# Two query tiles exchanged, the output projection's first part paced ahead of the attention, samples prepared beside the last head with their outputs outside the page pool

## The chip, the cores and the metric

The kernel runs as one program on 1 core of a Trainium2 chip. The metric is the device time of one execution in microseconds (us). TensorE (PE, with its weight loads PEld), VectorE (DVE), ScalarE (ACT), GpSimd (POOL) and SyncE (SP) each work through their own list of instructions in the order in which the program was written, and wait on semaphores for one another. SP issues most of the DMA transfers, ACT and POOL issue a few.

## The reference

One inference step of a two-layer hybrid encoder. Each layer projects its input, runs three mixers side by side (multi-head latent attention, an mLSTM and a gated delta net), gates their outputs, and projects the concatenation back:

```
proj = rms_norm(x, norm_w) @ w_in
q = (rms_norm(c_q, q_norm) @ w_uq).reshape(B, L, MLA_HEADS, MLA_NOPE + MLA_ROPE)
q_nope, q_rope = q[..., :MLA_NOPE], apply_rope(q[..., MLA_NOPE:], pos)
c_new = rms_norm(c_kv, kv_norm); kr_new = apply_rope(k_r, pos)
...
if absorbed:  q_lat = einsum('blhd,rhd->blhr', q_nope, w_uk)          # samples
else:         k_nope = einsum('bkr,rhd->bkhd', c_kv, w_uk); v = einsum('bkr,rhd->bkhd', c_kv, w_uv)   # prompt
p = softmax(where(mask, (q_rope·k_rope + q·k) * scale, -inf)) ; o = p · v   (samples: p · c_kv, then w_uv)
...
mixed = concatenate([o_a * silu(z_a), o_m * silu(z_m), o_g * silu(z_g)], axis=-1)
return x + mixed @ w_out, ...
```

There is one prompt of 16 + 1024 frames and there are 8 sample streams of 16 new frames, each with a cache of 1040 latent rows of 256 numbers and 1040 rope keys of 32. The 8 heads have 64 plain ("nope") and 32 rotated ("rope") query dimensions. Arithmetic is float32; products are made from a high and a low part of each operand, three matmuls for one.

## The kernel before, in words

All activations stand transposed, 1168 columns (1040 of the prompt, 128 of the samples) in three slices. SBUF is mostly a pool of 28 numbered "pages" (tiles named `pg`, 128 x 1168 float32 or thereabouts); smaller tiles (`wk`, `sm`) have pools of their own. PSUM has two pools, `pa` of 3 and `pb` of 5 buffers. `room(n)` asks whether n pages are free.

The order of all instructions is made when the program is built, by a planner (class `Weave`). A main thread writes the projections, then `qkv`, then `out_first` and `out_proj`; side threads (`prep`, `gload`, `att_m`, `att`, `samp_*`) yield either a time in planner microseconds after which they are resumed, or the name of an event that they wait for. When no side thread is due, the main thread writes its next piece, so its matmuls fill the places between the side threads' steps. A changed pause, page count or event therefore moves instructions on all engines.

Per layer, in the places that the change touches:

- `qkv`: `qtile(j)` makes the query tiles. Tiles 0 and 3 hold rope dimensions of four heads each: DVE multiplies the PSUM result with the two halves of a rotation table `tabq` (L1420, L1423), POOL adds them (L1425), SP writes 8 pieces to the scratch tensor `qS` in DRAM (L1435). Tiles 1, 2, 4 and 5 hold nope dimensions: ACT scales them out of PSUM (L1427), SP writes two pieces (L1438). Tile 0 comes first, then tile 1, then the four key tiles, written to `kS` by slices (L1458, L1459), then the values. `load` (L453) fetches the next weights `wuv` or `wuq`, which ACT and then DVE or POOL split (L437, L441). The event `("qt", g)` lets the side thread `gload` fetch a head's queries and keys from `qS` and `kS` (L383, tiles `pg`) and ACT and POOL or DVE split them (L1529, L1530).
- `att` goes over 8 heads, 3 query slices and up to 9 key blocks. A step is three score matmuls, an exponential on ACT (L1589) and, three steps later, the product with the values (PV) into a `pa` buffer. At the end of a slice DVE forms the reciprocal of the denominator (L1612) and multiplies by the gate (L1613), POOL multiplies the two (L1614), and ACT issues the store of the 64 x 320 or 64 x 384 result to the scratch tensor `mix` (L1616). Each step yields `YX` = 0.35.
- `out_first` is the output projection's part for four of the twelve tiles of `mix`: 8 blocks of rows by 3 slices, 12 matmuls each. It is the main thread's work while the attention runs.
- `samp_prep` waits for the eighth head's queries and keys (event `("grp", 7)`) and 9 free pages, turns the samples' queries into the latent space (16 matmuls and 16 splits with DVE subtractions L441, after the rope part L1645 and L1646), and takes two pages `OL` for the samples' outputs.
- For each of 8 samples b: `samp_load` fetches the transposed latent (2 pages `latT`, 520 KB each) and the rope keys `krT`, three copies in 96 rows (390 KB); `samp_split` splits them (ACT L1697, L1700; DVE and POOL L1698, DVE L1701); `samp_ln` fetches the latent once more, rows first (`latN`, two pages of 512 KB, after the small `latE` and `tok` pieces, L383); `samp_s` makes scores (21 matmuls of 352 columns), their extremes (DVE L1744) and exponentials (ACT L1752); `samp_t` transposes these (9 transposes at L372, copied out at L1776 and L1783) and multiplies by `latN` (36 matmuls, "PV of a sample"). The result is copied to `OL` at L1795.
- `samp_out` turns `OL` into the samples' attention output, and `out_proj` does the remaining eight tiles of the output projection.

A DMA instruction waits, beside its data, for the transfer that used its semaphore slot before it: hardware-queue transfers go through eight slots (`DMAHW0` to `DMAHW7`) in turn. A transfer whose slot is still taken holds SP, and all that SP has to issue after it.

Of the kernel before, what the change touches and what calls it, by code (L numbers as in the profile page):

```python
# [42 lines left out]
YM_, YX, YR, YD = 0.5, 0.35, 2.4, 2.6  # L43
# [111 lines left out]
def pack(i):  # L155
# [52 lines left out]
    a["krT"] = f(np.concatenate([kr.transpose(0, 1, 3, 2)] * 3, 2))  # L208
# [99 lines left out]
def _build(nc, tc, ctx, I, O, layers):  # L308
# [278 lines left out]
    def layer(l, XH, XLp, XL, xres, xw, R):  # L587
# [797 lines left out]
        def qkv():  # L1385
# [19 lines left out]
            def qtile(j, wh, wl):  # L1405
# [25 lines left out]
                if j in (0, 3):  # L1431
                    for h in range(4):
                        for x_ in range(2):
                            o = 64 * x_ + 16 * h
                            QE.dma_start(qS[4 * (j // 3) + h, 64 + 16 * x_:80 + 16 * x_], sg[o:o + 16, :T])  # L1435
                else:
                    for h in range(2):
                        QE.dma_start(qS[2 * gr + h, 0:64], sg[64 * h:64 * h + 64, :T])  # L1438
                    D1["qt", gr] = 1
                free(sg)  # L1440

            (wh, wl), nxt = nxt, load("k")
            yield from qtile(0, wh, wl)
            yield from qtile(1, wh, wl)
# [122 lines left out]
        def att():  # L1567
            steps = [(h, s_, j) for h in range(8) for s_ in range(3) for j in range(9) if QB[j] < QS_[s_][1]]
            fly, po, zt = [], None, {}
            for i_ in range(len(steps) + LA):  # L1570
# [46 lines left out]
                yield YX  # L1617
# [8 lines left out]
        def samp_prep():  # L1626
            yield "qs"
            yield ("grp", 7)
            while not room(9):
                yield 7.08  # L1630
# [10 lines left out]
            for a in range(2):  # L1641
# [4 lines left out]
                V.tensor_sub(dst[64:96], src[64:96], dst[64:96].bitcast(F32))  # L1646
# [14 lines left out]
            A["OL"] = [pg() for _ in range(2)]  # L1661
# [4 lines left out]
        def samp_load():  # L1666
            yield "sprep"
            fly = A["fly"] = []
            for b in range(8):
                for k in range(3):  # L1670
# [4 lines left out]
                    p_, src = (slice(0, 128), I["latT"][l, b, :, k]) if k < 2 else (slice(0, 96), I["krT"][l, b])  # L1675
# [5 lines left out]
        def samp_split():  # L1681
            for b in range(8):
                out = []
                for k in range(3):
# [9 lines left out]
                    for s0 in (0, 528):  # L1694
# [4 lines left out]
                        else:  # L1699
                            gate(S.copy(hi[0:96, sl], raw[0:96, sl]))  # L1700
                            V.tensor_sub(hi[32:64, sl], raw[32:64, sl], hi[32:64, sl].bitcast(F32))  # L1701
# [59 lines left out]
        def samp_t():  # L1761
            for b in range(8):
# [31 lines left out]
                for r in range(2):  # L1794
                    (S.copy if r else V.tensor_copy)(  # L1795
                        A["OL"][r][:, :1024].rearrange("p (h b l) -> p h b l", h=8, b=8)[:, :, b, :],
                        po[:, 128 * r:128 * r + 128].rearrange("p (h l) -> p h l", l=16))
# [3 lines left out]
        def samp_out():  # L1801
# [21 lines left out]
            for pr in range(4):  # L1823
                ps = pb()
                for j in range(2):
                    h = 2 * pr + j
                    for r in range(2):
                        mm(ps[64 * j:64 * j + 64, 0:128], wuv[:, 512 * r + 64 * h:512 * r + 64 * h + 64],
                           OL[r][:, 128 * h:128 * h + 128], r == 0, r == 1)
# [3 lines left out]
            free(wuv, zs, *OL)  # L1833
# [35 lines left out]
        def out_first():  # L1869
# [22 lines left out]
            for a, b_ in mx:  # L1892
                free(a, b_)

# [96 lines left out]
```

## Time and profile before

| | |
|---|---|
| median of 3 runs | 2653.65 us (2650.51 to 2656.03) |
| profiled execution, its own time | 2655.11 us |
| its span in the profile | 2653.3 us |
| TensorE's mean granted clock | 0.976 of 2.4 GHz |
| PE busy | 2494.3 us, 94% |
| PEld, DVE, ACT, POOL busy | 81%, 58%, 42%, 29% |
| moved by DMA | 258.67 MB, mean 97 GB/s |

The profiled execution is 1.46 us longer than the median, and 1.8 us of its time lie outside the span. PE is busy nearly throughout, so what another engine costs shows as a gap in PE's row; each gap carries the instruction that ended it. Layer 0's attention ends at about 1137 us of the span, layer 1's at about 2440 us. PE's busy time also grows when its clock is granted at the lower of its two levels, 1.2 instead of 2.4 GHz; the windows show this as a mean clock under 1.00, where a window of 20 us at clock c holds (1 - c) x 20 us of lost time.

### The profile page before, as it was taken

What the parts mean: (1) busy time and instruction counts of PE and PEld (TensorE: products, weight loads), DVE (VectorE), ACT (ScalarE), POOL (GpSimd) and SP (SyncE); (2) the same over time, 40 slices, a digit from 0 to 9 for tenths busy, and PEclk for the clock granted to TensorE, in tenths of its full rate; (3) what the DMA queues carried; (4) which work ended last, traced back from release to release, by engine and by line L of the source; (5) the groups of instructions that cost most, each with busy time, mean ns of one, the idle gap of its engine ahead of it and who ended that gap; (6) DMA issues with size and microseconds to landing.
All of it is one profiled execution on the core that took longest, in us unless ns stands there. A gap on an engine that the chain in (4) does not pass through costs nothing. (4 is left out here: it accounts for less than half of the span.)

```text
span 2653.3 us, 45522 instructions
## 1 busy us (share of the span) xinstructions
PE 2494.3 (94%) x17310; PEld 2154.2 (81%) x17310; DVE 1529.8 (58%) x3716; ACT 1115.5 (42%) x2635; POOL 763.2 (29%) x865
## 2 busy tenths in 40 slices
PE   6999999999999999979998999999999999999997
PEld 4887888878878888779977888788788788887896
DVE  6667465465453476655565784755743526665636
ACT  5363444444442433443343544444444434334612
POOL 3112222122123542232341222221221245322414
PEclk9999999999999999989999999999999999998998
DMA  3212112121113734464422121221211255444832
GB/s 130 67 40 76 51 52 83 51 69 49 60 59 113 201 105 122 124 215 160 153 79 57 43 74 52 61 73 51 69 52 57 84 148 162 116 115 149 281 117 80
DMA packets 158411, 258.67 MB, mean 97 GB/s; under 512 B 48704, under 2 KB 110768, under 8 KB 158192
## 3 DMA queue, kind: packets, MB, share of 16 engines
q1 hardware_dynamic: 152224, 247.59, 30.2%
q0 software_dynamic: 1856, 3.86, 0.7%
q10 hardware_dynamic: 4112, 4.30, 0.7%
q8 instruction: 137, 2.24, 0.4%
q14 instruction: 82, 0.67, 0.1%
HBM read 190.77 MB, written 64.92 MB: 96 GB/s over the span
## 5 line engine op out<-in xcount | busy, mean ns | idle before, releaser
L361 PE MATMUL pa<-pg,wh 128*128 128x384 f32 (+3 forms) x6324 | 1320.5, 352 | 25.5 <-DVE wk L1423 8.8
L361 PEld LDWEIGHTS pa<-pg,wh 128*128 128x128 f32 x6324 | 1108.2, 190 | 69.4 <-DVE wk L1423 9.4
L361 PE MATMUL pb<-pg,pg 128*128 128x352 f32 (+26 forms) x1908 | 427.4, 339 | 17.7 <-DVE sm L1552 4.4
L361 PE MATMUL pa<-pg,wb 128*128 128x384 bf16 (+1 forms) x2208 | 422.1, 331 | 6.2 <-POOL pg L544 4.2
L361 PEld LDWEIGHTS pb<-pg,pg 128*128 128x128 f32 (+7 forms) x1908 | 302.5, 189 | 71.1 <-issue 14.9
L361 PEld LDWEIGHTS <-wb 128*128 128x128 bf16 x2208 | 202.0, 98 | 142.4 <-issue 30.4
L361 PE MATMUL pb<-wk,pg 128*128 128x128 f32 (+4 forms) x2168 | 224.2, 250 | 21.2 <-ACT wk L983 5.5
L441 POOL TENSOR_TENSOR wh<-wf,wh 128x1024 fp32r<-128x1024 f32 (+1 forms) x61 | 144.1, 2363 | 325.1 <-ACT wh L437 318.7
L361 PEld LDWEIGHTS pb<-wk,pg 128*128 128x128 f32 (+3 forms) x2168 | 195.2, 162 | 43.0 <-issue 16.8
L1589 ACT ACTIVATE wk<-pb 128x320 f32<-128x320 f32 (+8 forms) x288 | 113.9, 406 | 244.9 <-PE pb L361 221.4
L361 PE MATMUL pa<-wk,pg 128*128 128x320 f32 (+8 forms) x576 | 192.5, 420 | 1.8 <-ACT wk L1589 1.3
L437 ACT CAST wh<-wf 128x1024 fp32r<-128x1024 f32 (+1 forms) x122 | 126.4, 1036 | 126.0 <-PE pa L361 110.7
L1552 DVE TENSOR_REDUCE sm<-pb 128x1 f32<-128x348 f32 (+9 forms) x232 | 107.8, 493 | 102.3 <-PE pb L361 89.6
L1612 DVE RECIPROCAL wk<-pa 64x320 f32<-64x320 f32 (+2 forms) x48 | 110.6, 2305 | 51.1 <-PE pa L361 50.4
L361 PE MATMUL pb<-wk,wk 32*32 32x16 f32 (+6 forms) x1776 | 110.7, 216 | 15.3 <-POOL wk L1285 5.6
L868 DVE SCALAR_TENSOR_TENSOR pg<-pg,vec,pg 128x1192 f32<-128x1192 f32 x72 | 107.2, 1504 | 18.3 <-ACT pg L866 18.0
L1530 POOL TENSOR_TENSOR pg<-pg,pg 64x520 fp32r<-64x520 f32 (+1 forms) x64 | 87.0, 1370 | 104.8 <-ACT pg L1529 91.1
L693 ACT COPY pg<-pa 128x384 f32<-128x384 f32 (+1 forms) x108 | 52.0, 481 | 134.4 <-PE pa L361 133.2
L457 ACT CAST wb<-wf 128x1024 bf16<-128x1024 f32 x92 | 96.2, 1045 | 26.3 <-PE pa L361 20.6
L441 DVE TENSOR_TENSOR wh<-wf,wh 128x1024 fp32r<-128x1024 f32 (+1 forms) x61 | 78.9, 1293 | 47.3 <-ACT wh L437 47.0
L361 PEld LDWEIGHTS pa<-wk,pg 128*128 128x128 f32 (+1 forms) x576 | 98.8, 195 | 5.9 <-ACT wk L1589 1.8
L361 PEld LDWEIGHTS pb<-wk,wk 32*32 32x32 f32 (+2 forms) x1776 | 73.2, 122 | 33.9 <-issue 9.4
(298 smaller groups left out, 3196.3 us busy)
## 6 DMA issues: line engine op xcount, KB each, us to landing
wf<-win SPq DMA_DIRECT2D x92, 512.0 KB
pg<-latT SPq DMA_DIRECT2D x32, 520.0 KB
pg<-latN SPq DMA_DIRECT2D x32, 512.0 KB
wf<-wout SPq DMA_DIRECT2D x24, 512.0 KB
xa<-wk SPq DMA_DIRECT2D x40, 192.0 KB
mix<-pg SPq DMA_DIRECT2D x12, 584.0 KB
pg<-mix SPq DMA_DIRECT2D x12, 584.0 KB
mix<-pg SPq DMA_DIRECT2D x12, 576.0 KB
```

Source lines behind the costliest of these rows:

```text
L361: W.last = P.matmul(out, lhsT, rhs, start=start, stop=stop)
L437: S.copy(hi, src)
L441: lo_eng.tensor_sub(lo, src, hi.bitcast(F32))
L457: S.copy(wb[:, :n], wf)
L693: S.copy(o[:, s0:s1], ps)
L868: V.scalar_tensor_tensor(y[:, :n], cb[:, j:j + n], vcol(l, "cw", 4 * ti + j), y[:, :n], op0=ALU.mult, op1=ALU.add)
L1530: G.tensor_sub(lo, raw, hi.bitcast(F32))
L1552: V.tensor_reduce(mx[:LEN[c], 3 * c + i_:3 * c + i_ + 1], ps[:LEN[c], :n1 - x_], axis=AX.X, op=ALU.min)
L1589: S.activation(pt[:m, :b - a], ps, AF.Exp, scale=-1.0)
L1612: V.reciprocal(rc, po[d, :w])
```

## The change

Four edits, all inside a layer:

1. `qtile(1)` is written before `qtile(0)`, and the event `("qt", 0)` is raised after tile 0, which is now the second.
2. `att` yields 0.55 instead of 0.35 after a step until `out_first` has ended.
3. `samp_prep` no longer waits for the eighth head, asks for 8 pages instead of 9, and keeps the samples' outputs in three `wk` tiles (two of 516 columns, one of 1024) in place of two pages; the copies to them become two on DVE and one on ACT instead of one each.
4. The rope keys of the samples come in two copies in 64 rows (260 KB) instead of three in 96, and the splits follow.

```diff
-YM_, YX, YR, YD = 0.5, 0.35, 2.4, 2.6
+YM_, YX, YR, YD, YF_ = 0.5, 0.35, 2.4, 2.6, 0.55
...
-    a["krT"] = f(np.concatenate([kr.transpose(0, 1, 3, 2)] * 3, 2))
+    a["krT"] = f(np.concatenate([kr.transpose(0, 1, 3, 2)] * 2, 2))
...
                     for h in range(2):
                         QE.dma_start(qS[2 * gr + h, 0:64], sg[64 * h:64 * h + 64, :T])
-                    D1["qt", gr] = 1
+                if j != 1:
+                    D1["qt", max(gr, 0)] = 1
                 free(sg)
             (wh, wl), nxt = nxt, load("k")
+            yield from qtile(1, wh, wl)
             yield from qtile(0, wh, wl)
-            yield from qtile(1, wh, wl)
...
-                yield YX
+                yield YX if "ofd" in D1 else YF_
...
         def samp_prep():
             yield "qs"
-            yield ("grp", 7)
-            while not room(9):
+            while not room(8):
                 yield 7.08
...
-                V.tensor_sub(dst[64:96], src[64:96], dst[64:96].bitcast(F32))
+                V.tensor_sub(dst[32:64], src[32:64], dst[32:64].bitcast(F32))
...
-            A["OL"] = [pg() for _ in range(2)]
+            H_ = [wt("H", 516) for _ in range(2)]
+            dg_ = wt("dg", 1024, 1, F32R).bitcast(F32)
+            A["OL"] = [[H_[h // 4][:, 128 * (h % 4):128 * (h % 4) + 128] for h in range(8)],
+                       [dg_[:, 128 * h:128 * h + 128] for h in range(8)]]
+            A["OLw"] = [[(H_[j][:, 0:512], 4 * j, 4) for j in range(2)], [(dg_, 0, 8)]]
...
-                    p_, src = ... (slice(0, 96), I["krT"][l, b])
+                    p_, src = ... (slice(0, 64), I["krT"][l, b])
...
-                            gate(S.copy(hi[0:96, sl], raw[0:96, sl]))
-                            V.tensor_sub(hi[32:64, sl], raw[32:64, sl], hi[32:64, sl].bitcast(F32))
+                            gate(S.copy(hi[0:64, sl], raw[0:64, sl]))
+                            V.tensor_sub(hi[64:96, sl], raw[0:32, sl], hi[0:32, sl].bitcast(F32))
...
                 for r in range(2):
-                    (S.copy if r else V.tensor_copy)(
-                        A["OL"][r][:, :1024].rearrange("p (h b l) -> p h b l", h=8, b=8)[:, :, b, :],
-                        po[:, 128 * r:128 * r + 128].rearrange("p (h l) -> p h l", l=16))
+                    for t_, h0, nh in A["OLw"][r]:
+                        (S.copy if r else V.tensor_copy)(
+                            t_.rearrange("p (h b l) -> p h b l", h=nh, b=8)[:, :, b, :],
+                            po[:, 128 * r + 16 * h0:128 * r + 16 * (h0 + nh)].rearrange("p (h l) -> p h l", l=16))
...
-            free(wuv, zs, *OL)
+            free(wuv, zs)
...
             for a, b_ in mx:
                 free(a, b_)
+            D1["ofd"] = 1
```

Three places of the new order, each of layer 1; layer 0 has the same. First SP, where the queries and keys go to the scratch tensors and the first head comes back (`qS`, `kS` are the scratch tensors, `pg` a page). Before:

```order
L383 DMA pg_22460<-tabq 128x1168 [waits DMAHW7_49,DMAHW6_49,PE_49]
L453 DMA wf_22565<-wuv 128x1024 [waits DMAHW1_49,DVE_49]
L1435 DMA qS<-pg_22474 16x1168 [waits Pool_49]
...
L1435 DMA qS<-pg_22474 16x1168 [waits DMAHW7_49]
L1438 DMA qS<-pg_22528 64x1168 [waits DMAHW0_49,Activation_49]
L1438 DMA qS<-pg_22528 64x1168 [waits DMAHW1_49]
L1459 DMA kS<-pg_22570 128x348 [waits DMAHW2_49,Activation_49]
...
L1459 DMA kS<-pg_22598 128x348 [waits DMAHW5_49,Activation_49]
L383 DMA pg_22609<-qS 96x1040 [waits DMAHW6_49,DMAHW0_49,PE_49]
L383 DMA pg_22611<-kS 64x1040 [waits DMAHW4_49,DMAHW7_49,DMAHW3_49,DMAHW2_49]
```

After (the lines from L1438 on stand one lower in the new code):

```order
L453 DMA wf_22574<-wuv 128x1024 [waits DMAHW1_49,DVE_49]
L1438 DMA qS<-pg_22483 64x1168 [waits Activation_49]
...
L1460 DMA kS<-pg_22579 128x348 [waits DMAHW2_49,Activation_49]
L453 DMA wf_22705<-wuq 128x768 [waits DMAHW7_49,DMAHW3_49,Pool_49]
L1435 DMA qS<-pg_22520 16x1168 [waits DMAHW4_49,Pool_49]
...
L1435 DMA qS<-pg_22520 16x1168 [waits DMAHW3_49]
L1460 DMA kS<-pg_22579 128x346 [waits DMAHW4_49,Activation_49]
L1460 DMA kS<-pg_22579 128x346 [waits DMAHW5_49,Activation_49]
L1460 DMA kS<-pg_22607 128x348 [waits DMAHW6_49,Activation_49]
L383 DMA pg_22618<-qS 96x1040 [waits DMAHW7_49,PE_49]
L383 DMA pg_22620<-kS 64x1040 [waits DMAHW5_49,DMAHW4_49,DMAHW0_49]
```

The two nope stores and one key store moved ahead of the eight rope stores (L1435), and so did the load of the next `wuq`, which waits for a POOL instruction (the subtraction L441 that splits `wuv`); the first head's load from `qS` still comes behind all eight rope stores.

Second, ACT at the end of the attention: `mix<-wk` is the store of a finished slice (L1616, now L1617), `pg<-pg` at L1697 and L1700 (now L1701, L1704) the splits of the samples' latent and rope keys, L1752 the exponentials of a sample, L1780 and L1787 the copies of transposes. Before:

```order
L1700 CAST pg_25248<-pg_25057 96x528
L1697 CAST pg_25254<-pg_25080 128x528 [waits DMASW2_49,DMASW0_49]
L1697 CAST pg_25254<-pg_25080 128x528
L1697 CAST pg_25261<-pg_25083 128x528 [waits DMAHW2_49]
L1697 CAST pg_25261<-pg_25083 128x528
L1700 CAST pg_25273<-pg_25086 96x528 [waits DMAHW3_49]
L1700 CAST pg_25273<-pg_25086 96x528
L1616 DMA mix<-wk_25174 64x320 [waits DMAHW0_49,Pool_49]
L1752 ACTIVATE pg_25333,wk_25304<-pb_25305,wk_25304 128x352 [waits DVE_49,PE_49]
L1752 ACTIVATE pg_25333,wk_25304<-pb_25314,wk_25304 128x352
L1752 ACTIVATE pg_25333,wk_25304<-pb_25323,wk_25304 128x352
L1697 CAST pg_25338<-pg_25245 128x528 [waits DMAHW2_49,PE_49]
```

After:

```order
L1701 CAST pg_25384<-pg_25289 128x528 [waits DMAHW4_49]
L1701 CAST pg_25384<-pg_25289 128x528
L1701 CAST pg_25391<-pg_25292 128x528 [waits DMAHW5_49]
L1701 CAST pg_25391<-pg_25292 128x528
L1704 CAST pg_25403<-pg_25295 64x528 [waits DMAHW6_49,DMASW5_49]
L1704 CAST pg_25403<-pg_25295 64x528
L1780 COPY wk_25452<-pa_25447 128x512 [waits PE_49,Activation_49]
L1787 COPY wk_25456<-pa_25454 128x128 [waits PE_49]
L1617 DMA mix<-wk_25304 64x320 [waits DMAHW3_49,Pool_49]
L1780 COPY wk_25521<-pa_25516 128x512 [waits PE_49,Activation_49]
L1787 COPY wk_25550<-pa_25548 128x128 [waits PE_49]
```

Before, the last store was followed by sample 0's exponentials, whose scores PE computes after the attention. Now the scores of samples 0 and 1 are written inside the attention (in layer 0 sample 0's were already), and the last store stands behind the copies of sample 0's transposes and ahead of those of sample 1.

Third, SP at the first `latN` loads of layer 1, `tok` and `latE` being the small pieces of the same pages. Before:

```order
L383 DMA pg_25245<-latT 128x1040 [waits DMASW3_49,DMAHW2_49,DMASW2_49,PE_49]
L383 DMA pg_25278<-latE 16x128 [waits DMAHW3_49,PE_49]
L383 DMA pg_25278<-tok 16x128 [waits DMAHW4_49]
L383 DMA pg_25279<-latE 16x128 [waits DMASW5_49,PE_49]
L383 DMA pg_25279<-tok 16x128 [waits DMAHW6_49]
L383 DMA pg_25278<-latN 128x1024
L383 DMA pg_25279<-latN 128x1024 [waits DMAHW1_49]
```

After:

```order
L383 DMA pg_25414<-latT 128x1040 [waits DMAHW4_49]
L383 DMA pg_25417<-latT 128x1040 [waits DMAHW5_49,PE_49]
L383 DMA pg_25420<-latE 16x128 [waits DMAHW6_49,PE_49]
L383 DMA pg_25420<-tok 16x128 [waits DMAHW7_49]
L383 DMA pg_25421<-latE 16x128 [waits DMAHW0_49,PE_49]
L383 DMA pg_25421<-tok 16x128 [waits DMAHW1_49]
L383 DMA pg_25420<-latN 128x1024 [waits DMAHW2_49]
L383 DMA pg_25421<-latN 128x1024 [waits DMAHW3_49]
```

The first half of sample 0's `latN` needs nothing new. The second half now waits for slot `DMAHW3`; the eight slots go round over SP's and ACT's transfers together, and the one that holds this slot before it is the last attention store on ACT's list above (in layer 1 before, the slot's holder was an earlier store). In layer 0 the first loads stood behind a late attention store already before.

## Rows read from the trace of the kernel before

**Rows 1.** Timeline of PE, projections of layer 1 (start, us, line, tiles, count, [idle<-releaser])
```profile
2161.26 18.03 PE L361 MATMUL pa<-pg,wh 128*128 128x400 f32 x99 [4.38 <-DVE wk L1423]
...
2181.10 1.19 PE L361 MATMUL pa<-wh,pg 128*128 128x512 f32 x4 [0.41 <-ACT pg L1458]
```

**Rows 2.** Timeline of DVE, query rope tile, layer 1
```profile
2160.05 3.49 DVE L1423 SCALAR_TENSOR_TENSOR wk<-pa,pg 64x400 f32<-64x400 f32 x6 [2.58 <-DMA pg<-tabq]
```

**Rows 3.** Timeline of SP, scratch stores of queries and their load, layer 1
```profile
2154.82 0.37 SPq L383 DMA_DIRECT2D pg<-tabq  x1
...
2173.28 0.37 SPq L383 DMA_DIRECT2D pg<-qS  x1
```

**Rows 4.** Timeline of POOL, split of wuv, layer 1
```profile
2169.39 2.40 POOL L441 TENSOR_TENSOR wh<-wf,wh 128x1024 fp32r<-128x1024 f32 x1 [0.60 <-ACT wh L437]
```

**Rows 5.** Timeline of ACT, first head split, layer 1
```profile
2180.08 0.63 ACT L1529 CAST pg<-pg 96x520 fp32r<-96x520 f32 x1 [2.21 <-DMA pg<-qS]
```

**Rows 6.** Windows of 20 us: busy of PE, PEld, DVE, ACT, POOL, then PEclk, DMA, GB/s
```profile
1140.00:1160.00 20.00, 9.37 (x45) 7.88 (x44) 12.41 (x18) 7.10 (x18) 9.93 (x16) 0.60 0.70 237
...
1160.00:1180.00 20.00, 16.74 (x106) 15.60 (x106) 9.15 (x16) 7.36 (x21) 4.35 (x8) 0.89 0.50 158
...
2160.00:2180.00 20.00, 18.74 (x103) 18.57 (x104) 3.36 (x6) 6.81 (x14) 7.76 (x9) 0.91 0.71 172
...
2400.00:2420.00 20.00, 17.45 (x70) 12.70 (x68) 8.15 (x20) 7.84 (x27) 1.72 (x6) 0.76 0.65 204
...
2420.00:2440.00 20.00, 20.00 (x100) 16.55 (x99) 10.35 (x9) 10.28 (x26) 5.41 (x6) 0.90 0.18 50
...
2440.00:2460.00 20.00, 17.40 (x95) 16.02 (x94) 14.84 (x28) 11.56 (x28) 8.10 (x15) 0.83 0.84 258
```

**Rows 7.** Timeline of PE, attention end of layer 0
```profile
1141.14 0.43 PE L361 MATMUL pb<-pg,pg 96*128 96x352 f32 x1 [0.69 <-DVE pg L1701]
...
1144.89 0.45 PE L372 MATMUL pa<-cst,pg 128*128 128x128 f32 x1 [2.21 <-DVE wk L1613]
...
1149.42 2.29 PE L372 MATMUL pa<-cst,pg 128*128 128x128 f32 x9 [4.08 <-ACT pg L1752]
...
1155.36 7.02 PE L361 MATMUL pb<-wk,pg 128*128 128x128 f32 x36 [3.65 <-DMA pg<-latN]
```

**Rows 8.** Waits of PE from 1136 to 1182 (total us, times, longest)
```profile
PE pa L372 <- ACT pg L1752: 7.1, 3, 4.1
```

**Rows 9.** Timeline of DVE, last attention division of layer 0
```profile
1137.43 2.15 DVE L1612 RECIPROCAL wk<-pa 64x320 f32<-64x320 f32 x1 [3.59 <-PE pa L361]
```

**Rows 10.** Timeline of POOL, same place
```profile
1140.46 1.30 POOL L1677 COPY pg<-sm 128x16 f32<-128x16 f32 x2
...
1141.73 1.30 POOL L1698 TENSOR_TENSOR pg<-pg,pg 128x528 fp32r<-128x528 f32 x1
...
1144.88 0.86 POOL L1614 TENSOR_TENSOR wk<-wk,wk 64x320 f32<-64x320 f32 x1 [1.85 <-issue]
```

**Rows 11.** Timeline of ACT's queue, last attention store of layer 0
```profile
1145.77 0.45 ACTq L1616 DMA_DIRECT2D mix<-wk  x1
```

**Rows 12.** Timeline of SP, first latN load of layer 0
```profile
1149.77 0.33 SPq L383 DMA_DIRECT2D pg<-tok  x1
...
1151.07 0.89 SPq L383 DMA_DIRECT2D pg<-latN  x2
```

**Rows 13.** Timeline of PE, sample preparation and attention end, layer 1
```profile
2409.85 6.33 PE L361 MATMUL pb<-pg,pg 96*128 96x320 f32 x21 [2.55 <-DVE pg L441]
...
2448.95 2.42 PE L361 MATMUL pb<-pg,pg 128*128 128x352 f32 x7 [2.35 <-ACT pg L1752]
...
2462.06 3.39 PE L361 MATMUL pb<-wk,pg 128*128 128x128 f32 x28 [1.32 <-ACT wk L1776]
```

**Rows 14.** Timeline of SP, first latN load of layer 1
```profile
2439.66 0.89 SPq L383 DMA_DIRECT2D pg<-latN  x2
```

**Rows 15.** Waits of PE from 1085 to 1112, sample preparation of layer 0
```profile
PE pb L361 <- DVE pg L441: 0.6, 1, 0.6
```

More of the change, by code (lines that the diff above doesn't have):

```diff
@@ L1674, in samp_load @@
                     fly.append(raw)
-                    p_, src = (slice(0, 128), I["latT"][l, b, :, k]) if k < 2 else (slice(0, 96), I["krT"][l, b])
+                    p_, src = (slice(0, 128), I["latT"][l, b, :, k]) if k < 2 else (slice(0, 64), I["krT"][l, b])
                     ld(raw[p_, :TP], src)
@@ L1828, in samp_out @@
                         mm(ps[64 * j:64 * j + 64, 0:128], wuv[:, 512 * r + 64 * h:512 * r + 64 * h + 64],
-                           OL[r][:, 128 * h:128 * h + 128], r == 0, r == 1)
+                           OL[r][h], r == 0, r == 1)
                 V.scalar_tensor_tensor(zs[:, 128 * pr:128 * pr + 128], ps[:, 0:128], 0.5, zs[:, 128 * pr:128 * pr + 128],
```

## The prediction

> **What bounds the kernel now.** I read the table of busy shares and then the windows. PE is busy nearly throughout, so the reader is to look only for windows where it is not, or where its clock is below 1.00, and to ask which wait ends last there. Three kinds of place lie inside the change. (a) Where the first query tile meets its rotation table: PE stops for 4.38 us and 18 us later for 0.41 us [rows 1], in layer 0 alike, and 1.8 us more go to the low clock (0.09 x 20 [rows 6]). (b) Layer 0's end of the attention: 0.69 + 2.21 + 4.08 + 3.65 = 10.6 us of idle PE [rows 7], after which two windows lose 8.0 and 2.2 us to the clock [rows 6]. (c) Layer 1: a stop of 2.55 us in the sample preparation, followed by 4.8 + 2.0 = 6.8 us lost to the clock, and stops of 2.35 and 1.32 us at the attention's end with 3.4 us lost [rows 13, 6]. All else of the span the change leaves in its order.
>
> **The exchange of the query tiles.** Removed: PE's wait for DVE's L1423, which itself waits 2.58 us for the second half of the table [rows 2]; the 27 matmuls of the nope tile, which needs no table, now lie in that wait (99 matmuls took 18.03 us, so 27 take 4.9 us [rows 1]). PE is then about 4.4 us early. What is late next: the first head's load. ACT's split of it stands ahead of two evacuations of the last key tile, it waits 2.21 us for the load already now, and PE's 0.41 us stop at 2181.10 is that evacuation [rows 5, 1]. The load is issued at 2173.28 [rows 3], behind all eight rope stores. They wait for POOL's last table addition, which waits for DVE, which waits for the table; its second half is issued at 2154.82 whatever the tiles' order [rows 3]. New in front of the rope stores on SP is the `wuq` load, which waits for POOL's `wuv` split (2.40 us, now done at 2171.8 [rows 4]); gone from behind them are the two nope stores and a key store. I find no row for the new issue time. It can come about 2.4 us later than now (the split wholly in front), or 4.4 us earlier (all of PE's lead passed on). PE's stop moves from the table to the evacuation, and what is won is what the load's issue wins: between -2.4 and +4.4 us, plus 1.8 us of clock at the upper end. I take 1.0 us for each layer, on the low side of the middle, since the table's arrival has not moved. Together -2.0 us.
>
> **The end of the attention.** In both layers sample 1's scores are now done inside the attention, and so are sample 0's in layer 1; their matmuls are the same, so this alone moves no time. PE then has 18 transposes (two of 2.29 us each [rows 7]) before it needs sample 0's `latN`. Its second half waits on SP for the slot of the last attention store. The chain, counted from the last attention matmul T: POOL has two splits (1.30 each), three small copies (0.65 each) and the product (0.86) [rows 10], 5.4 us, beginning when ACT's splits come; before, the store left 1145.77 - 1137.43 = 8.3 us after the reciprocal began [rows 9, 11]. Between 5.4 and 8.3 I take 6.7. The store needed 1149.77 - 1145.77 = 4.0 us until SP went on [rows 11, 12], and PE went on 1155.36 - 1151.07 = 4.3 us after `latN` was issued [rows 12, 7]. So PE goes on at T + 15.0, less 4.6 us of transposes: a hole of 10.4 us (9.1 to 12.0).
> The Trainium skill, page "DMA: Bandwidth & Descriptors", section "Anatomy of one DMA — SWDGE (gpsimd) path", puts a transfer at about 2.0 us fixed plus its bytes at 436 GB/s: by that, an estimate of 2.2 us for the store and 3.2 us for `latN`, the hole would be 7.5 us and the sum below 5.8 us smaller, over both layers. The rows' 4.0 and 4.3 us, from this place and with other loads under way, stand against it, and I go by the rows.
> Layer 0: +10.4 - 10.6 = -0.2. The two later stops of 1.53 us, in which transposes waited for exponentials (7.1 us in three, less 4.08, is 3.0 [rows 8]), go, because the product of sample 1 now follows sample 2's scores directly with its transposes long done: -3.0. With them goes the low clock after the first of them; I put 1.7 of the 2.2 us lost in that window [rows 6] on it and leave 0.5 to the end of the hole's own stretch: -1.7. Sum -4.9.
> Layer 1: before, `latN` was issued at 2439.66, ahead of the attention's end, and no store held it [rows 14]. So the hole is new: +10.4 - 2.35 - 1.32 = +6.7. The clock after a hole like layer 0's costs what it cost there, 8.0 + 0.5 = 8.5, in place of 3.4: +5.1. Sum +11.8.
>
> **The sample preparation.** It moves ahead of the last heads' attention in both layers and is interleaved with the row maxima of the last head, which also are DVE's. In layer 1 it cost 2.55 + 6.8 = 9.4 us; in layer 0 PE waited 0.6 us for the same splits, and no low clock followed [rows 13, 15]. Afterwards both layers have the same order: like layer 0's, the sum is 8.8 us smaller; like layer 1's, 8.8 us larger. By its cause layer 1's row is the nearer (the same wait, only longer), by the out_first matmuls that may lie beside it layer 0's. I take 0, between them, and keep both ends.
>
> **The rest at nothing.** The pause of 0.55 makes `out_first` end sooner and leaves a longer stretch of attention alone; in such a stretch PE had 20.00 of 20 us at 2420 to 2440 [rows 6], so this costs nothing as long as exponentials keep up. The smaller rope-key load saves 8 x 130 KB a layer and the split copies add eight small DVE copies, both beside a PE that is at work in the sample phase. If that cover were gone, eight copies like the nearest small one (0.65 us [rows 10]) would cost 5.2 us a layer, and 1.04 MB at the 258 GB/s of the window at 2440 [rows 6] would save 4.0 us; the two cancel to about 1 us.
>
> **Sum.** -2.0 - 4.9 + 11.8 + 0 + 0 = +4.9 us on the profiled execution: 2655.1 + 4.9 = 2660.0. That execution stands 1.46 us above the median of the runs, so I forecast 2653.65 + 4.9 = 2658.5 us for the median.
>
> **Rivals.**
> 1. The exchange holds in full: the load's issue passes all of PE's lead on. Then each layer wins 4.4 + 1.8 = 6.2 us, 12.4 in place of 2.0: 2658.5 - 10.4 = 2648.1, faster. For it: two stores fewer lie between the rope stores and the load. Against it: the load follows the table's arrival, and the split of `wuv` is now in front.
> 2. Layer 1 keeps its old end, because the store leaves early enough (POOL's splits done before T) that `latN` lands while the transposes run: the hole stays 3.7 us, with no new low clock. 2658.5 - 11.8 = 2646.7, faster. The point from which it decides is the store's issue: it must come by T (T + 4.6 + 3.7 - 4.0 - 4.3). Against it: DVE's reciprocal alone takes 2.15 us after T [rows 9].
> 3. Both: 2636.3.
> 4. The preparation stops PE in both layers and the clock falls in both: 2658.5 + 8.8 = 2667.3, slower. For it: DVE has the row maxima and the splits together there, and PE waited for these splits in both layers already.
> 5. The preparation runs smoothly in both: 2649.7, not told from no change.
> That the change doesn't reorder what it says is excluded by the order of the instructions.
>
> **How the numbers follow.** Chances: forecast 0.37, rival 1 0.14, rival 2 0.17, rival 3 0.08, rival 4 0.16, rival 5 0.08. A measurement of this kernel tells about 0.2% (5.3 us) from no change. The forecast's own range is 2652 to 2664 (the hole from 9.1 to 12.0 in each layer, 2.6 less to 3.2 more, and the exchange from -2.4 to +4.4): slower in 0.21 of its 0.37, no change in 0.16. Rival 1 splits 0.08 faster to 0.06 same, rival 2 0.12 to 0.05, rival 3 is faster, rival 4 slower, rival 5 0.02 faster, 0.06 same. Faster 0.30, same 0.33, slower 0.37. The range that leaves two in ten out reaches from rivals 1 and 2 with some room to rival 4: 2640 to 2670.
>
> **What would show it.** In the new profile: no stop at L1423, but one of 3 to 4 us at the key or value evacuation, behind the split of the first head (the exchange's step); PE waiting for `latN` by 10 us at the end of the attention in both layers with a window clock near 0.60 after it, and SP waiting for the last `mix<-wk` store there; in layer 0 no 1.53 us waits of the transposes. The forecast is wrong if layer 1's hole is under 5 us, if the first head's load is issued 3 us or more earlier against PE's work, or if the preparation shows stops in both layers or none.

## The result, and the profile after

The changed kernel takes 2671.31 us (median, 2667.51 to 2672.08) against 2652.08 us for the kernel before: ratio 1.0069, interval 1.0053 to 1.0085, so 18.3 us slower by the ratio (the medians differ by 19.2). Forecast were 4.9 us and a range up to 2670: the direction was right, the size not, and the time lies outside the range. The profiled execution of after took 2667.51 us, that of before 2655.11, so the two traces differ by 12.4 us, about 6 us less than the ratio says.

To find where they differ, I compare the time at which PE starts its n-th matmul in the two traces. The order agrees at three places of each layer: the begin of the queries, shortly before the samples' preparation, and after the samples' scores. The first stretch of a layer is head and attention, the second the tail. Windows of before, PE's busy time first, its clock third from the end:

```profile
827.00:1072.19 245.19, 234.97 (x1251) 209.38 (x1251) 135.77 (x213) 89.11 (x203) 102.50 (x115) 0.97 0.50 139
1072.19:1232.68 160.49, 140.69 (x851) 124.90 (x850) 94.36 (x150) 74.35 (x196) 51.41 (x72) 0.93 0.56 185
2103.29:2368.98 265.69, 256.92 (x1402) 228.25 (x1401) 143.07 (x218) 99.96 (x221) 106.78 (x116) 0.98 0.48 137
2368.98:2526.99 158.01, 146.12 (x853) 128.99 (x851) 94.94 (x152) 76.57 (x200) 52.38 (x79) 0.90 0.60 191
```

The same stretches of after:

```profile
822.20:1062.61 240.41, 231.41 (x1252) 207.28 (x1252) 132.30 (x211) 86.24 (x195) 96.82 (x110) 0.98 0.51 144
1062.61:1229.26 166.65, 141.72 (x851) 125.22 (x850) 100.50 (x158) 76.52 (x203) 54.65 (x78) 0.92 0.53 168
2102.22:2366.97 264.75, 255.54 (x1401) 227.63 (x1401) 139.72 (x218) 96.70 (x214) 104.57 (x113) 0.99 0.47 139
2366.97:2539.47 172.50, 149.68 (x852) 131.68 (x851) 102.58 (x158) 78.68 (x208) 58.49 (x81) 0.87 0.53 166
```

The heads are shorter by 4.8 and 0.9 us, the tails longer by 6.2 and 14.5 us. In the tails PE's idle time (length less busy) goes from 19.8 to 24.9 and from 11.9 to 22.8 us, and the clock's loss ((1 - clock) x length) from 11.2 to 13.3 and from 15.8 to 22.4 us. Of the 20.7 us by which the tails grow, 16.0 are idle time; the other 4.6 are PE's busy time, which is longer where its clock is low (the clock's loss lies partly in idle time, so it is not added to the stops). The stretches outside of heads and tails are 2.5 us shorter in the trace of after. So the loss is in the tails, of both layers, and mostly in stops.

The head first. PE at the query tiles of layer 1 after (answers to [rows 1]), then SP [rows 3] and POOL [rows 4]:

```profile
2162.57 10.73 PE L361 MATMUL pa<-pg,wh 128*128 128x346 f32 x66 [0.51 <-DVE wk L1423]
...
2177.57 7.22 PE L361 MATMUL pa<-wh,pg 128*128 128x512 f32 x24 [2.89 <-ACT pg L1459]
```

```profile
2153.88 0.37 SPq L383 DMA_DIRECT2D pg<-tabq  x1
...
2166.98 3.56 SPq L1435 DMA_DIRECT2D qS<-pg  x8
...
2172.68 0.34 SPq L383 DMA_DIRECT2D pg<-qS  x1
```

```profile
2163.58 2.40 POOL L441 TENSOR_TENSOR wh<-wf,wh 128x1024 fp32r<-128x1024 f32 x1
2165.94 1.01 POOL L1425 TENSOR_TENSOR pg<-pg,wk 128x384 f32<-128x384 f32 x1
```

The table's stop is 0.51 instead of 4.38 us, and a stop of 2.89 us (3.62 in layer 0) stands at the key tile's evacuation, ACT's L1459, behind the split of the first head. POOL does the `wuv` split in front of the third table addition; the rope stores start at 2166.98, later than before, and the load of the first head at 2172.68. That is 0.6 us earlier on the span, but 0.5 us later counted from the layer's begin of the queries (2102.22 after, 2103.29 before).

Now layer 0's tail, PE's stops (answers to [rows 7, 8, 15]):

```profile
1079.39 2.28 PE L361 MATMUL pb<-pg,pg 64*128 64x128 f32 x7 [4.48 <-DMA pg<-wukT]
...
1123.04 1.33 PE L361 MATMUL pb<-pg,pg 96*128 96x384 f32 x3 [3.46 <-ACT wk L1590]
...
1146.06 0.33 PE L372 MATMUL pa<-cst,pg 128*128 128x128 f32 x1 [2.87 <-ACT wk L1780]
...
1149.00 1.12 PE L372 MATMUL pa<-cst,pg 128*128 128x128 f32 x4 [1.14 <-DVE wk L1614]
1151.62 0.47 PE L372 MATMUL pa<-cst,pg 128*128 128x128 f32 x1 [1.50 <-ACT wk L1780]
...
1156.32 5.15 PE L361 MATMUL pb<-wk,pg 128*128 128x128 f32 x28 [2.51 <-DMA pg<-latN]
...
1193.52 0.43 PE L361 MATMUL pb<-pg,pg 96*128 96x352 f32 x1 [1.59 <-DVE pg L1705]
...
1204.84 0.43 PE L361 MATMUL pb<-pg,pg 96*128 96x352 f32 x1 [1.71 <-DVE pg L1705]
```

and layer 1's (answers to [rows 13]):

```profile
2390.55 3.75 PE L361 MATMUL pb<-pg,pg 64*128 64x128 f32 x16 [2.15 <-DVE pg L441]
...
2432.88 1.07 PE L361 MATMUL pb<-pg,pg 96*128 96x384 f32 x3 [2.92 <-ACT wk L1590]
...
2464.82 6.21 PE L361 MATMUL pb<-wk,pg 128*128 128x128 f32 x28 [2.50 <-DMA pg<-latN]
...
2503.08 0.43 PE L361 MATMUL pb<-pg,pg 96*128 96x352 f32 x1 [1.59 <-DVE pg L1705]
...
2514.42 0.43 PE L361 MATMUL pb<-pg,pg 96*128 96x352 f32 x1 [1.69 <-DVE pg L1705]
```

The hole at the attention's end is there in both layers: in layer 0 2.87 + 1.14 + 1.50 + 2.51, and 0.36 between, make 8.4 us, in layer 1 8.2. The transposes' waits of 1.53 us are gone. SP waits there for the last attention store, between the two halves of `latN`; the store leaves ACT at 1150.43, and the second half follows at 1152.46 (layer 0):

```profile
1145.44 7.37 SPq L383 DMA_DIRECT2D pg<-latN  x2
...
1150.43 0.45 ACTq L1617 DMA_DIRECT2D mix<-wk  x1
```

But three kinds of stop are new, which no term of the sum held: at the `wukT` load of the preparation (4.48, in layer 1 0.99), at an exponential late in the attention (3.46 and 2.92), and at the rope keys' split of the late samples (1.59 and 1.71 in layer 0, 1.59 and 1.69 in layer 1).

The first has this cause on SP:

```profile
1069.46 0.42 SPq L386 DMA_DIRECT2D xa<-wk  x1
1074.31 0.45 SPq L383 DMA_DIRECT2D wk<-mix  x1
1074.81 0.58 SPq L383 DMA_DIRECT2D pg<-wukT  x1
```

Between the store ending at 1069.88 and the gate load `wk<-mix` at 1074.31 SP waits 4.4 us for a `mix<-wk` store, and the `wukT` load stands behind. By the code the gate load overwrites one of two tiles (tag `Og`) from which these stores read, so it has to wait for the store of that tile. PE wants `wukT` at 1074.9.

The second, on DVE, POOL and ACT (ACTq is the store issued by ACT):

```profile
1115.66 2.16 DVE L1613 RECIPROCAL wk<-pa 64x320 f32<-64x320 f32 x1
1117.75 2.72 DVE L1702 TENSOR_TENSOR pg<-pg,pg 128x528 fp32r<-128x528 f32 x2
1120.50 0.48 DVE L1614 TENSOR_TENSOR wk<-pa,wk 64x320 f32<-64x320 f32 x1
```

```profile
1116.35 3.56 POOL L1702 TENSOR_TENSOR pg<-pg,pg 128x528 fp32r<-128x528 f32 x2 [1.90 <-issue]
1121.06 0.85 POOL L1615 TENSOR_TENSOR wk<-wk,wk 64x320 f32<-64x320 f32 x1 [1.15 <-DVE wk L1614]
```

```profile
1115.59 1.17 ACT L1701 CAST pg<-pg 128x528 fp32r<-128x528 f32 x2
1121.95 0.45 ACTq L1617 DMA_DIRECT2D mix<-wk  x1
1122.50 0.49 ACT L1590 ACTIVATE wk<-pb 128x384 f32<-128x384 f32 x1 [5.75 <-POOL pg L1681]
```

DVE divides, then does two splits of a sample (2.72 us) before it multiplies; POOL's two splits take 3.56 us; POOL's product ends at 1121.91; the store that ACT has next in its list goes at 1121.95, after 5.2 us in which ACT did nothing; the exponential that PE waits for starts at 1122.50, behind the store. (Its row puts the wait down to a small copy on POOL.) The samples' splits, more of which now stand between the attention's steps, hold a store, and the store holds ACT.

### The profile page after: what moved, and what is told of

Its sections match the earlier page's. It is cut to its first block, busy times and chain, and to the rows that moved or that the text cites. A ratio compares the mean times of both kernels' runs of the same rounds, so it can differ in the third digit from the quotient of the medians.

```text
span 2665.7 us, 45560 instructions
## 1 busy us (share of the span) xinstructions
PE 2492.6 (94%) x17310; PEld 2153.8 (81%) x17310; DVE 1537.5 (58%) x3732; ACT 1114.5 (42%) x2635; POOL 766.6 (29%) x865
## 5 line engine op out<-in xcount | busy, mean ns | idle before, releaser
L361 PE MATMUL pb<-pg,pg 128*128 128x352 f32 (+23 forms) x1844 | 425.1, 345 | 34.0 <-ACT wk L1590 7.4
L361 PEld LDWEIGHTS pb<-pg,pg 128*128 128x128 f32 (+6 forms) x1844 | 299.0, 192 | 92.5 <-issue 17.5
L361 PE MATMUL pb<-wk,pg 128*128 128x128 f32 (+5 forms) x2232 | 230.2, 252 | 21.4 <-ACT wk L983 6.0
L361 PEld LDWEIGHTS pb<-wk,pg 128*128 128x128 f32 (+4 forms) x2232 | 200.6, 162 | 42.9 <-issue 15.7
L441 POOL TENSOR_TENSOR wh<-wf,wh 128x1024 fp32r<-128x1024 f32 (+1 forms) x61 | 144.4, 2368 | 306.2 <-ACT wh L437 306.0
L361 PE MATMUL pb<-wk,wk 32*32 32x16 f32 (+6 forms) x1776 | 110.4, 216 | 13.3 <-DVE wk L1131 5.1
L868 DVE SCALAR_TENSOR_TENSOR pg<-pg,vec,pg 128x1192 f32<-128x1192 f32 x72 | 107.3, 1505 | 18.3 <-ACT pg L866 18.0
L441 DVE TENSOR_TENSOR wh<-wf,wh 128x1024 fp32r<-128x1024 f32 (+1 forms) x61 | 77.3, 1267 | 54.6 <-ACT wh L437 54.4
```

The source lines that it names most:

```text
L361: W.last = P.matmul(out, lhsT, rhs, start=start, stop=stop)
L441: lo_eng.tensor_sub(lo, src, hi.bitcast(F32))
L868: V.scalar_tensor_tensor(y[:, :n], cb[:, j:j + n], vcol(l, "cw", 4 * ti + j), y[:, :n], op0=ALU.mult, op1=ALU.add)
```

## The experiments

Each kernel was timed against the kernel before on the same chip; all ratios are to that.

**The query tiles alone.** Edit on the kernel before: the two `yield from qtile` lines swapped and the event raised after tile 0, nothing else.

> The kernel before with the two query tiles exchanged and nothing else. Theory: the stop at the table goes (4.4 us a layer) and one of about 3 us at the key tile's evacuation takes its place, behind ACT's split of the first head, so 1 to 2 us are won in each layer: 2 to 4 us faster, ratio 0.9985 to 0.9993. Rival (the exchange holds in full): 10 to 12 us faster, ratio about 0.996. Rival (the exchange is part of what was lost): slower than before, ratio over 1.001.

Ratio 0.9999 (0.9988 to 1.0009). No gain that can be told from none; the interval takes in the small end of the theory (0.9993) and excludes the full gain.

**The query tiles put back in the changed kernel.**

> The changed kernel with the query tiles in the old order. Theory: it loses the 1 to 2 us a layer that the exchange won, so it is 2 to 4 us slower than the changed kernel, ratio to before 1.0075 to 1.009. Rival: the exchange is part of the loss, ratio to before under 1.005.

Ratio 1.0110 (1.0096 to 1.0125): the exchange is worth about 11 us there, more than either theory allowed and more than alone. In its trace, 6.6 us longer than that of the changed kernel, the heads are longer by 3.5 and 1.1 us and the tails shorter by 2.4 us; the other 4.4 us lie in stretches that the edit leaves alone. Why the exchange is worth more there is open; it is no part of the loss.

**All attention stores from POOL's queue, in the changed kernel.**

```diff
-                        S.dma_start(mixS[8 + h // 2][r, q0:b], z)
+                        G.dma_start(mixS[8 + h // 2][r, q0:b], z)
```

> The changed kernel with every attention result stored by POOL's queue instead of ACT's, so that neither ACT's next exponential nor the hardware slot that the second half of latN needs waits for POOL's product. Theory: the stops of 3.46 and 2.92 us at exponentials late in the attention go, with 3 and 2 us of low clock after them, and of the hole at the attention's end (8.4 and 8.2 us) the parts that wait for latN and for ACT's copy behind the store (4.0 us in each layer) go: 14 to 20 us faster than the changed kernel, ratio to before 0.999 to 1.002. Rival (the stops are DVE's and POOL's backlog, and the queue that issues the store does not matter): at most 4 us faster than the changed kernel, ratio 1.005 to 1.007.

Ratio 1.0009 (0.9996 to 1.0021): 16 of the 18 us come back. PE's stops at the three places in layer 0:

```profile
1074.98 1.32 PE L361 MATMUL pb<-pg,pg 64*128 64x128 f32 x7 [2.65 <-DMA pg<-wukT]
...
1117.63 0.80 PE L361 MATMUL pb<-pg,pg 96*128 96x256 f32 x3 [1.41 <-ACT pg L1756]
...
1143.03 6.92 PE L361 MATMUL pb<-wk,pg 128*128 128x128 f32 x36 [0.59 <-DMA pg<-latN]
```

All three are shorter: 2.65 for 4.48, 1.41 for 3.46, 0.59 for 2.51. In layer 1 the late exponential and `latN` are shorter too (1.50 for 2.92, 1.22 for 2.50), but the stop at `wukT` is longer, 1.62 for 0.99. The first was not forecast. It comes from the order: with this edit SP's list has the `wukT` load ahead of the gate load, and it is issued 5.2 us earlier than in the changed kernel:

```profile
1069.65 0.42 SPq L383 DMA_DIRECT2D pg<-wukT  x1
```

SP's gate loads still wait for attention stores, though these no longer pass through SP's slots: 28.1 us of waits for `mix<-wk` between 1080 and 1240, against 42.5 in the changed kernel. Of the difference, 6.7 us is the wait of the second half of `latN` for the last store's slot, which is gone. So this run changes the queue and one place of SP's order together, and does not tell them apart.

**Single places of the same.** One store or load of each layer is moved to POOL's queue:

```diff
+ last store:   (G if (h, s_) == (7, 2) else S).dma_start(...)
+ one store:    (G if (h, s_) == (6, 2) else S).dma_start(...)
+ wukT:         ld(wkT[:, :1024], I["wukT"][l]..., G)
```

> The changed kernel with only the last attention result of each layer stored by POOL's queue. It tells the hole at the attention's end from the stops at the late exponentials, which it leaves as they are. Theory (two places, each with its own price): of the hole go the waits for latN (2.5 us) and for ACT's copy behind the store (1.5 us), 4 us in each layer, perhaps with some low clock: 6 to 10 us faster than the changed kernel, ratio to before 1.003 to 1.005. Rival (the late exponentials alone make the difference that the POOL stores made): the ratio stays at 1.006 to 1.007. Rival (the hole alone makes it): the ratio falls to 1.000 to 1.002.

> The changed kernel with a single store of each layer, that of the seventh head's last slice, issued by POOL's queue; the list of every other engine is unchanged but for that one row. It is the store that ACT held for 5.75 us in layer 0 while exponentials stood behind it. Theory: the stops of 3.46 and 2.92 us and the low clock after them (3.4 and 1.8 us) go, 8 to 12 us faster than the changed kernel, ratio to before 1.002 to 1.004. Rival (the exponentials are late for another reason, DVE's and POOL's splits): at most 2 us, ratio over 1.006.

> The changed kernel with the samples' wukT load issued by POOL's queue instead of SP's. Theory (the preparation's stop is SP's list held by an attention store in front of that load): the stops of 4.48 and 0.99 us at that load shrink to under 1 us and some of the low clock after them goes: 3 to 7 us faster than the changed kernel, ratio to before 1.004 to 1.006. Rival (the preparation stops for its splits anyway): no difference, 1.0065 to 1.0075.

Last store: 1.0062 (1.0040 to 1.0083), about 2 us. The interval takes in the slow end of the first theory (1.004 to 1.005) as well as the first rival, so it excludes only that the hole alone makes the loss. In its trace the stop for `latN` is gone in both layers, and that for ACT's copy is 0.73 instead of 1.50 us. One store: 1.0069 (1.0050 to 1.0088), nothing: my theory that this held store by itself makes the loss fell. PE's stop there in the run:

```profile
1126.09 1.01 PE L361 MATMUL pb<-pg,pg 96*128 96x256 f32 x3 [2.48 <-ACT pg L1756]
```

It is 2.48 instead of 3.46 us and is now ended by a sample's exponential (L1756): with the store away, the samples' chain on DVE is next in the same place (ACT waits 3.56 us there for DVE's extremes). `wukT`: 1.0039 (1.0024 to 1.0054), 8 us back, the stop in layer 0 0.61 instead of 4.48 us:

```profile
1078.10 1.32 PE L361 MATMUL pb<-pg,pg 64*128 64x128 f32 x7 [0.61 <-DMA pg<-wukT]
```

In layer 1 that stop grows from 0.99 to 2.95 us, against the expectation, while the 2.15 us behind it (DVE's L441) go. PE's idle time in the two tails falls by about 4 us; where the rest of the 8 us comes from is not shown.

**Two complements.** The three places together, and all stores except the two.

> The changed kernel with three transfers of each layer issued by POOL's queue: the wukT load, the seventh head's last store and the last store. Theory A (the three places make the loss): as good as with all stores from POOL, ratio to before 1.000 to 1.002. Theory B (each attention store holds SP's loads through its slot, and these three are only the last of them): the wukT load's 8 us and the last store's 2 us and little more, ratio 1.002 to 1.005.

> The changed kernel with all attention stores from POOL's queue except the seventh head's last and the last one, which ACT issues as before. Theory B (the stores hold SP, and with it the loads of wukT and of the samples, all along the attention): most of the 16 us comes back, ratio to before 1.001 to 1.003. Theory A (those two stores and the wukT load make it): about what the wukT load alone brought, ratio 1.003 to 1.006.

Three places: 1.0033 (1.0021 to 1.0046), hardly more than `wukT` alone, as theory B had it. All stores but the two: 1.0032 (1.0019 to 1.0044), an interval that takes in parts of both theories' ranges. Neither theory has it alone: each set brings about 9.5 us, all stores 16. The second set has the same place of `wukT` on SP as all stores.

**The pace, the event, the pages and the rope keys of the changed kernel undone one at a time.**

```diff
- YF_ = 0.55                      + YF_ = 0.35                      (old pace)
-                                 + yield ("grp", 7)                (samp_prep waits again)
- H_, dg_ as outputs, room(8)     + A["OL"] = [pg() for _ in range(2)], room(9)   (pages)
- [kr...] * 2, 64 rows            + [kr...] * 3, 96 rows            (rope keys)
```

> The changed kernel with the attention's pause at 0.35 throughout. Theory (the samples' splits between the attention's steps lose the time, whatever the pace): ratio to before 1.005 to 1.008, with stops of about 3 us at late exponentials. Rival (ending out_first early takes away the matmuls that covered the waits): ratio under 1.002.

> The changed kernel with the samples' preparation waiting for the eighth head's load again, the rest of the change kept. Theory: what was lost came from the samples moving into the attention, so the stop at the wukT load (4.5 us in layer 0) and those at the late exponentials go, and the old end of the attention comes back: ratio to before 0.998 to 1.002. Rival (the pace of out_first, the pages or the rope keys lose the time): the ratio stays at 1.005 to 1.008.

> The changed kernel with the samples' outputs in two pages again and 9 pages asked for, the rest of the change kept. In its order the scores of samples 0 and 1 stand behind the attention again. Theory (the two freed pages are what lets the samples' splits into the attention, and these hold the attention's stores): the stops of about 3 us at the late exponentials go, ratio to before 0.998 to 1.003. Rival (the earlier preparation or the rope keys lose the time by themselves): the ratio stays over 1.004.

> The changed kernel with the rope keys in three copies in 96 rows again; the order of every engine stays as it is, only these transfers and splits are larger or differ in rows. Theory: the late stops at the rope keys' split (1.6 and 1.7 us in each layer) come from its place behind two latent splits on DVE, not from its form: they stay, and 130 KB more for each sample cost 0 to 3 us, ratio to before 1.0065 to 1.0085. Rival (reading 32 rows and writing others makes DVE's subtraction slower, 0.94 us in the late samples against 0.67): the ratio falls to 1.003 to 1.005.

Old pace: 1.0009 (0.9994 to 1.0025). The rival's number came, but the traces don't bear out its reason. `out_first`'s last matmuls stand ahead of the preparation's first ones in every trace counted for this (before, after and seven of the runs), so they cover none of the samples' splits. In layer 0, before, after, and with the old pace (the preparation after starts at 1079.39, shown above):

```profile
1089.88 0.77 PE L361 MATMUL pa<-pg,wh 128*128 128x384 f32 x3
1099.03 1.30 PE L361 MATMUL pb<-pg,pg 64*128 64x128 f32 x7
...
1064.55 0.77 PE L361 MATMUL pa<-pg,wh 128*128 128x384 f32 x3
...
1085.68 0.77 PE L361 MATMUL pa<-pg,wh 128*128 128x384 f32 x3
1094.85 1.31 PE L361 MATMUL pb<-pg,pg 64*128 64x128 f32 x7
```

What the longer pause does is to end `out_first` some 20 us sooner. `out_first` frees eight pages at its end, which is the number that `samp_prep` asks for, and in these traces the preparation follows that end by 4 to 15 us. So the preparation moves forward with it, and the samples' splits move into the attention. The casts of these splits that ACT does before the attention's last matmul, in layers 0 and 1: 12 and 7 before, 18 and 18 after, 16 and 5 with the old pace. That the preparation waits for the pages is read from the code and not tested by itself. Before, all of layer 1's seven casts begin between 2420 and 2440, the first two here:

```profile
2420.74 1.15 ACT L1697 CAST pg<-pg 128x528 fp32r<-128x528 f32 x2
```

With the old pace the stop at `wukT` is gone in layer 0, and no stop from there to the attention's end is over 1.3 us. In layer 1 the samples' first scores stand behind the attention again, with a stop of 3.55 us there; the late rope-key stop stays (layer 0's in the second line):

```profile
2439.86 0.75 PE L361 MATMUL pb<-pg,pg 96*128 96x352 f32 x3 [3.55 <-DVE pg L1705]
...
1190.59 0.43 PE L361 MATMUL pb<-pg,pg 96*128 96x352 f32 x1 [1.62 <-DVE pg L1705]
```

Waiting for the eighth head: 1.0064 (1.0050 to 1.0078), the theory fell: the samples still stand inside the attention (18 and 18 casts), and the event is not what keeps them out. Outputs in pages: 1.0007 (0.9986 to 1.0029), as expected; without the two pages the samples' first scores stand behind the attention (7 and 7 casts), though the stop at `wukT` is still there in layer 0 (4.03 us). Its profiled execution was 0.8% over its median; of it I read only the stops ahead of the late samples' matmuls, as the costliest groups have them (busy time and mean, then the idle time and what ended most of it):

```profile
L361 PE MATMUL pb<-pg,pg 96*128 96x352 f32 x48 | 16.8, 350 | 1.6 <-DVE pg L1701 1.2
```

and beside it the same group with the old rope keys, whose order is the changed kernel's:

```profile
L361 PE MATMUL pb<-pg,pg 96*128 96x352 f32 x48 | 15.9, 339 | 6.6 <-DVE pg L1705 6.6
```

The stops are gone with the pages, and stay with the old keys. Rope keys: 1.0070 (1.0057 to 1.0083): their new form costs and saves nothing that this can tell (some 3 us), in an order that is otherwise the same.

**What the runs point to.** The stores from POOL's queue on the kernel before, alone; with the exchange; with exchange and `wukT`; and on the changed kernel with the old pace.

> The kernel before with all attention results stored by POOL's queue, the query tiles in the old order. With the run that also exchanges the tiles it tells the two gains apart. Theory: the stores make most of it (the hole at layer 0's end), ratio 0.9965 to 0.9985. Rival (the exchange makes it, once SP is no longer held): ratio 0.9985 to 1.000.

> The kernel before with the query tiles exchanged and all attention results stored by POOL's queue: what the runs point to as a better version. Theory: the 10.6 us hole at the end of layer 0's attention loses the wait for the last store's slot (4 us and more) and some of its low clock, the exchange wins 0 to 4 us: 5 to 12 us faster, ratio 0.9955 to 0.998. Rival (the samples' order of before does not depend on who stores): ratio 0.9985 to 1.001.

> The kernel before with the query tiles exchanged, all attention stores from POOL's queue and the wukT load from POOL's queue. Theory: in the old order the wukT load has time (no stop at it before), so this equals the version without it, ratio 0.995 to 0.9975. Rival (freeing SP of that load helps the samples' loads): ratio under 0.995.

> The changed kernel with all attention stores from POOL's queue and the old pause of 0.35. Theory (the held stores and the missing out_first matmuls are two halves of one stop, so that taking away the second brings little more): ratio 0.996 to 1.000. Rival (they add): ratio under 0.995.

Alone 0.9978 (0.9969 to 0.9988); with the exchange 0.9962 (0.9948 to 0.9976); with `wukT` too 0.9955 (0.9940 to 0.9971), not told from the former; the last, the changed kernel with stores from POOL and the old pace, 1.0021 (1.0008 to 1.0034), worse than expected, so the two cures of the changed kernel do not add. The second beats both kernels by 10 and 28 us. Its end of layer 0's attention:

```profile
1142.33 2.29 PE L372 MATMUL pa<-cst,pg 128*128 128x128 f32 x9 [4.22 <-ACT pg L1753]
1144.96 3.72 PE L361 MATMUL pb<-wk,pg 128*128 128x128 f32 x16 [0.34 <-DMA pg<-latN]
```

The stop for `latN` is 0.34 instead of 3.65 us [rows 7]; the stop for exponentials before it stays.

## Why the prediction was wrong, point by point

By stretches the forecast was -2.0 us for the heads, -4.9 for layer 0's tail and +11.8 for layer 1's. The traces have -5.7, +6.2 and +14.5. So most of the miss that the traces show is layer 0's tail, where the stops that no term held make 4.48 + 3.46 + 3.30 = 11.2 us; in layer 1 they make 7.2.

- *The pause costs nothing as long as exponentials keep up; of the samples' scores, their matmuls are the same, so this alone moves no time:* this is the step that failed. I moved the samples' matmuls and priced nothing of what comes with them: per sample six casts on ACT and six subtractions on DVE and POOL, in lists that also carry the attention's division, product and store. The stretch that I named as cover, with PE at 20.00 of 20 us [rows 6], held all seven casts of samples in that attention; now an attention has 18. The pause was no bystander: it frees the pages sooner and so brings the preparation and the splits forward. With the old pause, or with the outputs in pages, nearly all of the loss is gone (1.0009 and 1.0007 for 1.0069).
- *The exchange, -2.0 us, a stop of 3 to 4 us behind the first head's split:* the mechanism was right (2.89 and 3.62 us at L1459, the rope stores behind the `wuv` split). Its size alone is within 3 us of nothing, as forecast; inside the changed kernel it was some 11 us, which stays unexplained.
- *The hole, 10.4 us in both layers:* right in mechanism and place, held `latN` and all, 8.4 and 8.2 in size. The clock after it in layer 1, forecast to cost 8.5 us, cost 8.6 (0.84 and 0.73 in the two windows from 2440 to 2480). That the sizes came so near is partly luck, since two terms were off and made up for each other. The store left 8.1 us after the last attention matmul (T, 1142.31 in layer 0) and not 6.7; SP went on 2.0 us after the store and not 4.0, in both layers; the 2.2 us that I had worked out and set aside was nearer. PE waited for `latN` by 2.5 us only; most of the hole is the copies of the transposes, behind splits and behind the store on ACT. What the hole is worth stays unclear: without the last store's wait the kernel was about 2 us faster, which is not told from nothing.
- *The preparation, 0 within 8.8:* it stopped PE in both layers, which the prediction had named as a sign of being wrong. Layer 0 stopped by 4.48 us, for a load and not for the splits that I had bounded it with; issuing that load from POOL was worth 8 us over both layers. The rule to list each DMA of a moved step, and what stands before it on SP, would have shown it: SP's list after has the gate load in front.
- *The late samples:* no stop forecast, 3.3 us in each layer measured. They stay with the rope keys' old form and go with the old order of the pages. The split's place is shown, what sets it is not.
- *The chances:* slower was the likeliest, at 0.37. All rivals but one were built on gains, and the one that was slower had one place; the range ended at it. The forecast's own range was also too narrow for its terms: the ends named there add to 2649.1 and 2668.5, not 2652 and 2664.

What stays open: how the 16 us of the stores divide between ACT, which waits for POOL's product, SP, which waits for the stores, and the earlier place of `wukT`. The runs show all three, and that single stores do not carry it.

## What to carry to other kernels

When a change lets one stage's work into another, price its casts and subtractions on the engines whose lists it joins, not its matmuls. An engine that issues a store of another engine's result waits for that result with everything behind it; try issuing it from the engine that makes the result. A filler that ends earlier saves nothing by itself; ask what waits for the pages that it frees, and where that work will then stand.

## What the runs showed of the hardware

An attention store issued by POOL took 0.59 us of its list (median of 48), against 0.45 on ACT, and yet moving all 48 of them to POOL made both kernels faster, by 16 and 6 us. From the issue of the last attention store (80 KB) until the transfer behind it in its slot could be issued took 4.0 us in layer 0 before and 2.0 us in both layers after.

In the profiled executions the clock's loss differs by more than the changes are worth: a tail's mean granted clock lay between 0.98 (layer 1, the combined kernel: 2.9 us lost) and 0.85 (layer 0, all stores but two: 25.7 us). A single trace therefore shows where PE stops, and the ratio over many executions shows what that is worth.
